# A transformer trunk on one core, split into two parts: all projections first, then attention and routing pair by pair in a new order

## The chip, the cores and the metric

The kernel runs on one core of a Trainium2 chip. The metric is the device time of one execution in microseconds (us), as the median of several runs. All times below are in us unless marked ns. TensorE multiplies matrices, VectorE and ScalarE work on elements, GpSimd here issues gathers of rows, and SyncE issues the other transfers, in the order of the program.

## The reference

One layer of a decoder is computed for a prompt of 1024 positions and for 8 sample rows of one position each, in float32. The model width is 1024.

```python
h = rmsnorm(x, norm_mix) * (1 + sc1) + sh1          # sc, sh, g: six rows of silu(c) @ w_ada + b_ada
qa, ka, va, ub, vb, xr, xg = split(h @ w_in)        # 1024 x 2560: q, k, v 512 each, the rest 256 each
ya = dilated attention of rmsnorm(q), rmsnorm(k), v # 8 heads x 64, three dilations, causal, relative bias
yb = spatial gating of ub by vb, chunks of 128
yc = gelu(xg) * linear recurrence of conv(xr)       # carries a state from one position to the next
x  = x + g1 * ([rms(ya) | rms(yb) | rms(yc)] @ w_out)
h2 = rmsnorm(x, norm_ffn) * (1 + sc2) + sh2
q2 = rmsnorm(h2 @ w_q)                              # 1024 x 2048: 8 heads, two halves of 128
for each head: the top 16 of 128 keys on each half, then the top 16 of their sums
               -> 128 experts e and gates w for every position
x  = x + g2 * sum_k w_k * gelu(h2 . u_tab[e_k]) * v_tab[e_k]   # tables of 16384 rows x 1024
```

## The kernel before, in words

**Tiles.** The prompt is cut into 8 tiles of 128 positions (0 to 7). The 8 sample rows are a ninth tile, `NT`. The trunk takes the tiles in the groups `(0, 1), (2, 3), (4, 5, NT), (6, 7)`. For each group `project(grp)` normalizes x, multiplies it with the five 512-column blocks of `w_in` (line 551, by `product`, lines 233 to 247), and makes queries, keys, values, the gating mixer and the recurrent mixer of it. It loads each block of `w_in` once for the group, so 4 x 20 loads of 512 KB. Keys and values go to tensors in device memory (`kT_d`, `vt_d`); queries and the mix stay on chip. Then `mix_and_route(grp, first)` runs attention for pairs of heads (`attention`, lines 591 to 625: logits at L606, weighted values at L623), the output projection with `w_out` (L695), the second norm, the router's product with `wq` (L728), the scores against the keys and the top 16 (`top16`). With the first group it also computes the remaining conditioning rows (`ada`, lines 185 to 213; the matmuls are L195 and L197), and with the third the sample rows' attention over their cache (`sample_attention`, lines 814 to 889).

**Experts.** Two ways lead through the experts. The tiles in `GATHER` fetch the rows of their 128 experts for each position: `peer_prompt` issues 128 fetches of 128 rows of `u_tab` and 128 of `v_tab`, each 512 KB, on GpSimd (L897); VectorE multiplies and adds them (L905, L914). The fetched rows take five buffers (`grow`). The tiles in `DENSE` go through all 16384 experts with matmuls in `dense()`, behind the trunk: 128 blocks of keys, each loading 512 KB of both tables, in 32 groups of four blocks (scores L1003, products L1019), with a table of gates that `gate_table` has built for each of these tiles (matmuls L805, ScalarE L804 and L807, VectorE L797) and stored to device memory.

**Order.** The code names neither semaphores nor times. A scheduler in front of the chip fixes one order of instructions for each engine, by the program's order as priority and by when operands are estimated to be ready. `pump` puts pieces of selection and gate tables of earlier dense tiles between the steps of attention and routing. The fetches of `peer_prompt` come last in the program and so fill what is free; a tile can be fetched once `select` has stored its experts. The next group's projection may run beside the routing of the group before. `Stream` objects hold the buffers: `Z` for projection, `R` for attention and routing together, each with two PSUM banks for products and some for the rest (`BANKS`), and both share seven buffers for weights (`WB`).

Of the kernel before, what the change touches and what calls it, by code (L numbers as in the profile page):

```python
# [23 lines left out]
GATHER = (0, 2, 6, 7)  # L24
DENSE = (1, 3, 4, 5)
GROUPS = ((0, 1), (2, 3), (4, 5, NT), (6, 7))
# [4 lines left out]
BANKS = dict(za=2, zs=1, ra=2, rs=2, g=1)  # L31
GST = 8
LK = 2
# [5 lines left out]
A4 = 3  # L39
WB = 7  # L40
# [20 lines left out]
def kernel(ctx: ExitStack, tc: tile.TileContext, I, O):  # L61
# [7 lines left out]
    mm = fctx.enter_context(tc.tile_pool(name="mm", bufs=1, space=PSUM))  # L69
    fc = fctx.enter_context(tc.tile_pool(name="fc", bufs=1))  # L70
    sm = fctx.enter_context(tc.tile_pool(name="sm", bufs=2))
    fr = fctx.enter_context(tc.tile_pool(name="fr", bufs=2))

    class Stream:


        def __init__(self, key, rows):
            self.key, self.rows = key, rows

        def ps(self, name="ps", kind="s"):  # L80
            return mm.tile([P, 512], F32, tag="p" + self.key + kind, name=name, bufs=BANKS[self.key + kind])

        def load_w(self, src):
            ws = []
            for j in range(4):
                w = fr.tile([P, 2, 512], F32, tag="w", name="w", bufs=WB)
                S.dma_start(w, src[j])
                ws.append(w)
            return lambda c: ws[c // 2][:, c % 2, :]

        def a2(self, name, dt=F32):
            return fr.tile([P, 512], dt, tag="a2" + self.key, name=name, bufs=self.rows)

        def junk(self):
            return fr.tile([P, D], BF, tag="a2" + self.key, name="junk", bufs=self.rows)

        def small(self, n, nm, bufs=2):
            return sm.tile([P, n], F32, tag=f"{nm}{n}{self.key}", name=nm, bufs=bufs)

    Z = Stream("z", 4)  # L100
    R = Stream("r", 4)

    def a4(name):
        return fr.tile([P, D], F32, tag="a4", name=name, bufs=A4)

    def c2(n, name):
        return fr.tile([P, 2, n], F32, tag="c2", name=name, bufs=2)

    def c1(n, name):
        return fr.tile([P, 2, n], F32, tag="c1", name=name, bufs=5)  # L110
# [5 lines left out]
    io_i = R.a2("io_i", I32)[:, :P]  # L116
    G.iota(io_i, pattern=[[1, P]], base=0, channel_multiplier=-1)
    V.tensor_scalar(ident, io_i, 0.0, None, op0=ALU.is_equal)
    tril = R.a2("tril")[:, :P]
# [10 lines left out]
    qgs = fc.tile([P, 1], F32, name="qgs")  # L130
    V.tensor_scalar(qgs, col("qg"), 0.125, None, op0=ALU.mult)
    bah = fc.tile([P, 4], F32, name="bah")
# [3 lines left out]
    xlast = fc.tile([P, 2, 3], F32, name="xlast")  # L136
    hlast = fc.tile([P, 2, 1], F32, name="hlast")
# [32 lines left out]
    cT = R.a2("cT")[:, :72].rearrange("p (c n) -> p c n", c=8)  # L170
    S.dma_start(cT, I["cT"])
    one32 = fc.tile([1, 32], F32, name="one32")
    V.memset(one32, 1.0)
    sc = fc.tile([P, 8, 32], F32, name="sc")
    sg_ = R.a2("se")[:, :72].rearrange("p (c n) -> p c n", c=8)
# [51 lines left out]
    def chunks(key, t):  # L227
        x = fr.tile([P, 8, wide(t)], F32, tag=f"hT{key}{wide(t)}", name="hT", bufs=2 if t < NT else 1)
# [21 lines left out]
    kgr = fc.tile([P, 64], F32, name="kgr")  # L250
    gnr = fc.tile([P, 256], F32, name="gnr")
    sp4 = fc.tile([P, 2], F32, name="sp4")
    nsp4 = fc.tile([P, 2], F32, name="nsp4")
    wsT = fc.tile([P, 4, P], F32, name="wsT")
    gw = fc.tile([P, 4, P], F32, name="gw")
    rb = fc.tile([33, 8, 8], F32, name="rb")
# [3 lines left out]
    def small_weights():  # L260
# [3 lines left out]
        nl, ab, u, z, z2, acc = (fc.tile([P, 2], F32, name=nm) for nm in ("nl", "ab", "lu", "lz", "lz2", "lacc"))  # L264
# [16 lines left out]
        wst = R.a2("wst").rearrange("p (g i) -> p g i", g=4)  # L281
# [8 lines left out]
    def bias_table():  # L290
        V.memset(rb, 1.0)
        rbs = fc.tile([32, 8], F32, name="rbs")
        S.dma_start(rbs, I["rel_bias"])
        V.tensor_copy(rb[:32], rbs[:, None, :].to_broadcast([32, 8, 8]))
        for q in range(3):
            ohq = R.a2("oh")[:33, :384]
            S.dma_start(ohq, I["oh"][:, q * 384:(q + 1) * 384])
            ps = R.ps("psr")
            T.matmul(ps[:8, :384], rb[:, 0, :], ohq, start=True, stop=True)
            rrow = R.a2("rrow")[:8, :384]  # L300
# [161 lines left out]
    def mixer_b(t, r, z, mix):  # L462
# [5 lines left out]
        if t == NT:  # L468
            S.dma_start(O["gv_s"], gv[:8])
            w0 = fr.tile([8, 8], F32, tag="w0", name="w0", bufs=1)  # L470
# [16 lines left out]
    def mixer_c(t, z, mix):  # L487
        if t == NT:
            S.dma_start(O["conv_s"][:, 2, :], z[:8, 0:256])
            S.dma_start(O["conv_s"][:, 0:2, :], I["state_conv"][:, 1:3, :])  # L490
            xps = fr.tile([P, 2, 4, 8], F32, tag="xps", name="xps", bufs=1)
            S.dma_start(xps[:, :, 0:3, :], I["state_convT"])
            xgs, h0 = (fr.tile([P, 2, 8], F32, tag=nm, name=nm, bufs=1) for nm in ("xgs", "h0"))
# [43 lines left out]
    qT, mix = {}, {}  # L537

    def project(grp):
        hT = {}  # L540
        for t in grp:
            r = rows_of[t]
            hT[t] = chunks("z", t)
            mix[t] = fr.tile([P, D], F32, tag="mix", name="mix", bufs=4)
            S.dma_start(mix[t][:r], x_src(t))
            normed_T(Z, t, r, mix[t], modT["sc1"], modT["sh1"], hT[t])
        for nb in (4, 0, 1, 3, 2):
            w = Z.load_w(I["w_in"][nb])
            for t in grp:
                r = rows_of[t]  # L550
                ps = product(Z, t, hT[t], w)
                z = Z.a2("z")
                A.copy(z[:r], ps[:r])
                if nb == 2:
                    if t == NT:
                        S.dma_start(O["v_s"], z[:8])
                        S.dma_start(v_d, z[:8])
                    else:
                        S.dma_start(O["v_p"][t * P:(t + 1) * P, :], z)
                        S.dma_start(vt_d[:, :, t, :].rearrange("h p e -> p h e"), z.rearrange("p (h e) -> p h e", h=4))  # L560
                elif nb == 0:
# [67 lines left out]
    def mix_and_route(grp, first):  # L629
        if first:  # L630
            ada(R, "g1")
# [550 lines left out]
```

## Time and profile before

| | us |
|---|---|
| median of three runs | 3331.42 |
| lowest, highest | 3325.81, 3339.45 |
| the profiled execution's own time | 3339.45 |
| its span, first to last instruction | 3337.4 |
| TensorE busy in the span | 2804.2 (84 %) |
| VectorE busy | 2542.5 (76 %) |
| GpSimd busy | 1405.2 (42 %) |
| ScalarE busy | 1197.8 (36 %) |
| moved by DMA | 952.57 MB, 285 GB/s on average |

In the rows below PE is TensorE's matmuls, PEld its weight loads, DVE VectorE, ACT ScalarE, POOL GpSimd and SPq SyncE's queue; `out<-in` are the program's names of tiles and tensors, and what stands behind a last arrow ended the idle time.

A busy share is an average over stages with different limits; matmuls are pipelined and their ends are modelled. The profile also gives the granted clock of TensorE as a share of its full speed (0.894 over the span).

### The profile page before, as it was taken

To read this page: it belongs to the slowest core of one execution; us is meant where nothing else is said; L and a number is where in the kernel's file an instruction comes from. 1 tells how busy PE (TensorE), PEld (TensorE's weight loads), DVE (VectorE), ACT (ScalarE), POOL (GpSimd) and SP (SyncE) were. 2 spreads that over 40 slices of the span, in tenths; PEclk is the share of its full clock that TensorE was granted. 3 is DMA by queue.
4 is the path that set the end of the run, shared out by engine and by line. 5 is a ranking of instruction groups with operands and counts; after the bars stand their busy time and mean duration, and the time that the engine had idled before them with its cause. 6 is when DMAs were issued, how large, how long until landed. Compare 5 with 4: busy or idle time off the path is not lost.

```text
span 3337.4 us, 36012 instructions
## 1 busy us (share of the span) xinstructions
PE 2804.2 (84%) x11152; PEld 1898.0 (57%) x11152; DVE 2542.5 (76%) x5342; ACT 1197.8 (36%) x2704; POOL 1405.2 (42%) x1046
## 2 busy tenths in 40 slices
PE   7989968856487788977768998989999989999989
PEld 3434445422145334555437876777777777777767
DVE  2216967897657788877798897888988888988974
ACT  4413566342137334575543221222222322222321
POOL 0000234414423543133423664666656466656540
PEclk9979988878577799898779999999999999999999
DMA  7665788938967888678886998999999899999983
GB/s 263 203 195 169 269 270 294 373 130 301 297 196 247 322 298 272 208 247 295 270 279 229 337 338 313 346 331 353 332 334 336 325 332 355 333 337 346 346 293 100
DMA packets 340670, 952.57 MB, mean 285 GB/s; under 512 B 35575, under 2 KB 118062, under 8 KB 338430
## 3 DMA queue, kind: packets, MB, share of 16 engines
q0 software_dynamic: 149760, 545.33, 46.3%
q1 hardware_dynamic: 190718, 404.95, 35.3%
q8 instruction: 88, 1.44, 0.2%
q14 instruction: 104, 0.85, 0.1%
HBM read 894.04 MB, written 60.85 MB: 286 GB/s over the span
## 4 chain that ended last, share of the span: by engine, by line
PE 27%; DMA 23%; issue 19%; DVE 14%; POOL 13%; ACT 4%; SPq 0%; POOLq 0%; DVEq 0%; ACTq 0%
POOL grow L897 13%; DMA grow<-in_peer_v,ge 9%; PE psz L238 7%; PE psG L805 4%; PE psO L1019 3%; PE psS L1003 3%; DMA grow<-in_peer_u,ge 3%; DVE acc L914 3%; DMA g_d<-st 3%; PE pso L623 2%; DVE grow L905 2%; PE pst L163 2%; PE lg L606 1%; DMA vt<-vt_d 1%; DMA vc<-in_cache_v 1%
## 5 line engine op out<-in xcount | busy, mean ns | idle before, releaser
L897 POOL DMA_INDIRECT grow<-in_peer_u,ge x520 | 697.3, 1341 | 1168.3 <-DVE grow L905 491.3
L897 POOL DMA_INDIRECT grow<-in_peer_v,ge x520 | 707.3, 1360 | 669.1 <-DVE acc L914 426.7
L914 DVE SCALAR_TENSOR_TENSOR acc<-grow,dot,acc 128x1024 f32<-128x1024 f32 x515 | 659.8, 1281 | 127.3 <-DMA grow<-in_peer_v,ge 120.9
L905 DVE SCALAR_TENSOR_TENSOR grow<-grow,gx 128x1024 f32<-128x1024 f32 x520 | 626.0, 1220 | 146.8 <-DMA grow<-in_peer_u,ge 116.2
L238 PE MATMUL psz<-w,hT 128*128 128x512 f32 x1408 | 673.5, 619 | 12.4 <-DVE hT L328 5.5
L238 PEld LDWEIGHTS psz<-w,hT 128*128 128x128 f32 x1408 | 261.8, 198 | 285.9 <-issue 261.9
L1019 PE MATMUL psO<-vh,ah 128*128 128x512 f32 x512 | 224.7, 439 | 125.4 <-DVE acc L1028 125.2
L972 ACT CAST vh<-v 128x1024 fp32r<-128x1024 f32 x128 | 125.3, 1049 | 504.7 <-PE psO L1019 502.6
L805 PE MATMUL psG<-o,oh 128*128 128x128 f32 x1024 | 204.7, 336 | 75.6 <-ACT st L807 66.0
L805 PEld LDWEIGHTS psG<-o,oh 128*128 128x128 f32 x1024 | 167.4, 229 | 148.5 <-ACT st L807 98.8
L797 DVE TENSOR_TENSOR oh<-iof,tr 128x1024 f32<-128x1024 f32 x128 | 156.4, 1224 | 98.6 <-PE psG L805 96.0
L972 ACT CAST ah<-a 128x512 fp32r<-128x512 f32 x128 | 79.7, 622 | 404.3 <-DVE a L1008 404.3
L972 ACT CAST uh<-u 128x1024 fp32r<-128x1024 f32 x128 | 135.0, 1055 | 232.5 <-PE psS L1003 229.8
L1019 PE MATMUL psO<-vl,ah 128*128 128x512 f32 x512 | 218.1, 426 | 0.0
L1019 PE MATMUL psO<-vh,al 128*128 128x512 f32 x512 | 216.1, 422 | 0.0
L1019 PE MATMUL psK<-vh,al 128*128 128x512 f32 x512 | 200.1, 391 | 9.8 <-DVE al L973 9.8
L804 ACT ACTIVATE o<-oh,tr 128x128 f32<-128x128 f32 x512 | 185.2, 400 | 45.7 <-PE psG L805 42.0
L1019 PEld LDWEIGHTS psO<-vh,ah 128*128 128x128 f32 x512 | 108.0, 211 | 164.6 <-DVE acc L1028 140.8
L1019 PE MATMUL psK<-vh,ah 128*128 128x512 f32 x512 | 199.8, 390 | 0.0
L1019 PE MATMUL psK<-vl,ah 128*128 128x512 f32 x512 | 199.7, 390 | 0.0
L973 DVE TENSOR_TENSOR ul<-u,uh 128x1024 fp32r<-128x1024 f32 x128 | 156.1, 1220 | 9.3 <-ACT uh L972 4.8
L973 DVE TENSOR_TENSOR vl<-v,vh 128x1024 fp32r<-128x1024 f32 x128 | 150.6, 1219 | 1.2 <-ACT vh L972 1.0
(369 smaller groups left out, 5024.2 us busy)
## 6 DMA issues: line engine op xcount, KB each, us to landing
u<-in_peer_uT SPq DMA_DIRECT2D x128, 512.0 KB
v<-in_peer_v SPq DMA_DIRECT2D x128, 512.0 KB
w<-in_w_in SPq DMA_DIRECT2D x80, 512.0 KB
w<-in_wq SPq DMA_DIRECT2D x64, 512.0 KB
g_d<-st SPq DMA_DIRECT2D x64, 512.0 KB
gc<-g_d SPq DMA_DIRECT2D x16, 2048.0 KB
w<-in_w_ada SPq DMA_DIRECT2D x48, 512.0 KB
w<-in_w_out SPq DMA_DIRECT2D x32, 512.0 KB
```

The costliest lines, as they stand in the source:

```text
L163: T.transpose(pv[:, c, :r], src[:, (c0 + c) * P:(c0 + c + 1) * P], ident[:r, :r])
L238: T.matmul(ps, xT[:, c, :], w(c), start=(c == 0), stop=(c == 7))
L797: V.tensor_tensor(oh, iof[:, None, None, :].to_broadcast([P, 2, OHB, P]), tt[:, 0:2, b * TB + n0:b * TB + n0 + OHB, None].to_broadcast([P, ...
L804: A.activation(o1, oh[:, 0, n0 % OHB + q, :], AF.Copy, scale=tt[:, 2, n:n + 1])
L805: T.matmul(ps[:, q * P:(q + 1) * P], oh[:, 1, n0 % OHB + q, :], o1, start=True, stop=True)
L897: G.indirect_dma_start(out=rt, out_offset=None, in_=tab, in_offset=bass.IndirectOffsetOnAxis(ap=idx, axis=0))
L905: V.scalar_tensor_tensor(rt, rt, 1.0, x, op0=ALU.mult, op1=ALU.mult, accum_out=w[:, k:k + 1])
L914: V.scalar_tensor_tensor(acc, rt, w[:, k:k + 1], acc, op0=ALU.mult, op1=ALU.add)
L972: A.copy(hi, x)
L973: eng.tensor_tensor(lo, x, hi, op=ALU.subtract)
L1003: T.matmul(ps[:, :n1 - n0], us_[x][:, j, :], xs_[j][y][:, n0:n1], start=(j == 0 and q == 0), stop=(j == 7 and q == 2))
L1019: T.matmul(ps, aa[x][:, t * P:(t + 1) * P], vv[y][:, hf * 512:(hf + 1) * 512], start=(k == 0 and (first or o not in keep)), stop=(k == 3 * ...
```

## The change

The trunk is split into two parts that have buffers and PSUM banks of their own.

The first part projects all nine tiles, one after the other, with the 20 pieces of `w_in` loaded once and kept in 20 buffers. All conditioning rows and the sample rows' attention are computed between the projections. Queries, and the half of the mix that the gating and recurrent mixers make, are now stored to device memory (`qT_d`, `mix_d`, `ya_d`) and loaded again by the second part.

The second part takes the groups in the order `(0, 1), (6, 7), (4, 5, NT), (2, 3)`. Attention has a stream of its own, `Y`. The banks are now two for logits and two for the rest of attention, one for routing products (two before), two for the rest of routing, one for gate tables. Keys, values and the router's keys have two buffers each (one before), the bias rows four (two before). The gathered tiles are 0 to 3 and the dense ones 4 to 7.

```diff
-GATHER = (0, 2, 6, 7)
-DENSE = (1, 3, 4, 5)
-GROUPS = ((0, 1), (2, 3), (4, 5, NT), (6, 7))
+GATHER = (0, 1, 2, 3)
+DENSE = (4, 5, 6, 7)
+GROUPS = ((0, 1), (6, 7), (4, 5, NT), (2, 3))
-BANKS = dict(za=2, zs=1, ra=2, rs=2, g=1)
+BANKS = dict(za=3, zs=3, xs=1, xv=1, aa=2, **{"as": 2}, ra=1, rs=2, g=1)
+TBB = 4
-A4 = 3
-WB = 7
+A4 = 4
+WZ = 6
+WB = 8
...
-    Z = Stream("z", 4)
-    R = Stream("r", 4)
+    first = Part("z")
+    Z = Stream(first, "z", 5)
+    X = Stream(first, "x", 4)
+    zp = first.fr
...
-    def project(grp):
+    def project(t):
...
         for nb in (4, 0, 1, 3, 2):
-            w = Z.load_w(I["w_in"][nb])
-            for t in grp:
+            if nb not in w_in:
+                w_in[nb] = Z.load_w(I["w_in"][nb], "wi", 20)
+            w = w_in[nb]
...
+                    qt = Z.a2("qT").rearrange("p (h n) -> p h n", h=4)
+                    transposes(Z, z, P, 4, lambda c0, pv: A.activation(qt, pv, AF.Copy, scale=qgs))
+                    S.dma_start(qT_d[t], qt)
...
+        S.dma_start(mix_d[t], mix[:r, 512:1024])
...
+    def mix_and_route(grp):
...
+        for t in grp:
+            mix[t] = fr.tile([P, D], F32, tag="mix", name="mix", bufs=4)
+            S.dma_start(mix[t][:rows_of[t], 512:1024], mix_d[t])
+            if t == NT:
+                S.dma_start(mix[t][:8, 0:512], ya_d)
+            else:
+                qT[t] = fr.tile([P, 4, P], F32, tag="qT", name="qT", bufs=2)
+                S.dma_start(qT[t], qT_d[t])
...
-            kT = fr.tile([P, D], F32, tag="kT", name="kT", bufs=1)
+            kT = fr.tile([P, D], F32, tag="kT", name="kT", bufs=2)
...
-            vt = fr.tile([P, NT, P], F32, tag="vt", name="vt", bufs=1)
+            vt = fr.tile([P, NT, P], F32, tag="vt", name="vt", bufs=2)
...
     ada(Z, "sc1")
     ada(Z, "sh1")
     small_weights()
+    project(0)
     bias_table()
+    project(1)
+    project(NT)
+    project(2)
+    sample_attention()
+    project(3)
+    ada(Z, "g1")
+    project(4)
+    ada(Z, "sc2")
+    project(5)
+    ada(Z, "sh2")
+    project(6)
+    project(7)
+    ada(Z, "g2")
+    first.close()
+    second = Part("r")
+    R = Stream(second, "r", 5)
+    Y = Stream(second, "a", 4)
...
     for i, grp in enumerate(GROUPS):
-        project(grp)
+        mix_and_route(grp)
+        pump(99)
         while late:
             now(select(late.pop()))
-        mix_and_route(grp, i == 0)
-        pump(99)
```

## Rows read from the trace of the kernel before

**Rows 1.** Stretches: busy us (count) of PE, PEld, DVE, ACT, POOL; clock, DMA, GB/s

```profile
core 0 of [0], span 3337.4 us
...
0.00:340.00 340.00, 298.73 (x997) 131.22 (x998) 115.51 (x601) 121.89 (x337) 0.63 (x6) 0.90 0.64 207
340.00:690.00 350.00, 283.56 (x1065) 160.49 (x1065) 283.35 (x855) 182.21 (x503) 143.29 (x117) 0.89 0.86 303
690.00:1040.00 350.00, 219.62 (x752) 104.92 (x751) 244.71 (x585) 123.08 (x314) 117.55 (x91) 0.72 0.70 227
1040.00:1355.00 315.00, 261.82 (x914) 130.19 (x912) 255.02 (x843) 136.42 (x394) 136.39 (x102) 0.88 0.84 290
1355.00:1716.00 361.00, 283.85 (x1287) 184.48 (x1286) 279.57 (x674) 213.25 (x619) 128.81 (x101) 0.85 0.77 254
1716.00:1771.00 55.00, 35.78 (x148) 29.02 (x149) 54.81 (x203) 30.52 (x38) 1.56 (x1) 0.79 0.78 260
1771.00:3188.00 1417.00, 1290.51 (x5437) 1051.64 (x5436) 1223.63 (x1485) 357.50 (x456) 853.69 (x612) 0.95 0.92 333
```

**Rows 2.** Fetches on GpSimd (L897): duration ns min/median/max, first and last start

```profile
L897 POOL DMA_INDIRECT grow<-in_peer_u,ge x520: 932/1299/4036, 358.7 to 3227.9; - x174
L897 POOL DMA_INDIRECT grow<-in_peer_v,ge x520: 932/1144/7060, 764.3 to 3242.3; - x174
```

**Rows 3.** SyncE's timeline, end of the span: start, duration, transfer

```profile
3204.97 0.34 SPq L923 DMA_DIRECT2D out_xp<-acc  x1
...
3296.68 0.34 SPq L954 DMA_DIRECT2D out_xs<-fin  x1
```

**Rows 4.** Waits from 340 to 1716: who for whom, us, times, longest

```profile
POOL grow L897 <- DMA ge<-e_d: 369.1, 2, 357.4
POOL grow L897 <- DVE grow L905: 320.5, 105, 32.0
```

**Rows 5.** DMA issues on the page: count, size

```profile
w<-in_w_in SPq DMA_DIRECT2D x80, 512.0 KB
```

**Rows 6.** TensorE's lines, 0 to 1716: count, busy us, mean ns, idle before

```profile
L238 PE MATMUL psz<-w,hT 128*128 128x512 f32 x1408 | 673.5, 619 | 12.4 <-DVE hT L328 5.5 <-DVE hss L337 3.3 <-DMA w<-in_w_in 2.4
...
L195 PE MATMUL psa<-w,sc 128*32 128x512 f32 x192 | 48.1, 755 | 14.7 <-DVE sc L180 10.9 <-DMA w<-in_w_ada 3.8
...
L163 PE MATMUL pst<-ident,mix 128*128 128x128 f32 (+1 forms) x144 | 31.0, 343 | 41.8 <-ACT hT L330 22.5 <-ACT mix L670 12.0 <-ACT mix L317 7.0
L872 PE MATMUL psv<-vc,pz 128*64 128x512 f32 (+1 forms) x32 | 30.0, 1070 | 32.2 <-DMA vc<-in_cache_v 31.9 <-ACT pz L865 0.3
L242 PE MATMUL psz<-w,hT 128*32 128x512 f32 x176 | 28.9, 642 | 3.1 <-DVE hss L337 3.1
...
L197 PE MATMUL psa<-brow,one 1*32 1x512 f32 x24 | 15.5, 732 | 0.0
...
L354 PE MATMUL psg<-xc,gw 128*128 128x128 f32 (+1 forms) x72 | 12.2, 315 | 10.5 <-DVE xc L350 10.5
```

**Rows 7.** The chain that ended last: start, duration, instructions

```profile
45.65 3.78 PE psz L238 x4
...
219.94 27.01 PE psz L238 x62
...
3248.79 21.76 PE psS L1003 x96
```

**Rows 8.** Logit matmuls (L606): duration ns, first and last start, shapes

```profile
L606 PE MATMUL lg<-kT,qT x192: 272/589/1219, 135.0 to 1465.2; 64*128 64x512 f32 x96, 64*128 64x128 f32 x32, 64*128 64x256 f32 x32, 64*128 64x384 f32 x32
```

**Rows 9.** Lines of all engines, 340 to 1716, columns as before

```profile
L905 DVE SCALAR_TENSOR_TENSOR grow<-grow,gx 128x1024 f32<-128x1024 f32 x256 | 309.9, 1218 | 51.1 <-DMA grow<-in_peer_u,ge 49.5 <-DMA gx<-h_d 0.8
...
L914 DVE SCALAR_TENSOR_TENSOR acc<-grow,dot,acc 128x1024 f32<-128x1024 f32 x148 | 188.8, 1276 | 30.7 <-DMA grow<-in_peer_v,ge 29.6
...
L730 ACT COPY q<-psz 128x512 f32<-128x512 f32 (+1 forms) x28 | 16.3, 582 | 50.4 <-PE psz L238 38.9 <-PE psz L246 6.5 <-DVE tkw L379 3.7
...
L697 DVE TENSOR_TENSOR tmp<-psz,g1r 128x512 f32<-128x512 f32 (+1 forms) x14 | 9.6, 685 | 9.3 <-PE psz L238 8.5 <-DMA g1r<-mods_g 0.5 <-PE psz L246 0.4
```

More of the change, by code (lines that the diff above doesn't have):

```diff
@@ L227, in chunks @@
     def chunks(key, t):
-        x = fr.tile([P, 8, wide(t)], F32, tag=f"hT{key}{wide(t)}", name="hT", bufs=2 if t < NT else 1)
+        x = (zp if key == "z" else R.fr).tile([P, 8, wide(t)], F32, tag=f"hT{wide(t)}", name="hT", bufs=2 if t < NT else 1)
         if t == NT:
@@ L247, in product @@
         return ps
[L250 to L256, printed above, removed]
+    kgr = zp.tile([P, 64], F32, name="kgr")
+    gnr = zp.tile([P, 256], F32, name="gnr")
+    sp4 = zp.tile([P, 2], F32, name="sp4")
+    nsp4 = zp.tile([P, 2], F32, name="nsp4")
+    wsT = zp.tile([P, 4, P], F32, name="wsT")
+    gw = zp.tile([P, 4, P], F32, name="gw")
+    rb = zp.tile([33, 8, 8], F32, name="rb")
     rb_d = dpool.tile([8, 1152], F32, name="rb_d")
@@ L616, in attention @@
             h_ = 2 * hp + hh
-            nmx = sm.tile([P, 1], F32, tag="nmx", name="nmx", bufs=4)
+            nmx = R.fr.tile([P, 1], F32, tag="nmx", name="nmx", bufs=4)
             A.activation(nmx, mx[hh], AF.Copy, scale=-1.0)
             A.activation(p_[hh][:, :nk], p_[hh][:, :nk], AF.Exp, bias=nmx, accum_out=sums[:, h_:h_ + 1])
-            pT = [R.a2("pT").rearrange("p (c q) -> p c q", c=4) for _ in range(0, t + 1, 4)]
-            transposes(R, p_[hh][:, :nk], P, t + 1, lambda c0, pv: A.copy(pT[c0 // 4][:, :pv.shape[1], :], pv))
+            pT = [Y.a2("pT").rearrange("p (c q) -> p c q", c=4) for _ in range(0, t + 1, 4)]
+            transposes(Y, p_[hh][:, :nk], P, t + 1, lambda c0, pv: A.copy(pT[c0 // 4][:, :pv.shape[1], :], pv))
             for c in range(t + 1):
@@ L627 @@
     tv = {}
-    def mix_and_route(grp, first):
-        if first:
-            ada(R, "g1")
+    def mix_and_route(grp):
+        fr = R.fr
         pt = [t for t in grp if t < NT]
-        if NT in grp:
-            sample_attention(mix[NT])
-        sums = {t: sm.tile([P, 8], F32, tag="sums", name="sums", bufs=4) for t in pt}
+        mix = {}
+        for t in grp:
+            mix[t] = fr.tile([P, D], F32, tag="mix", name="mix", bufs=4)
+            S.dma_start(mix[t][:rows_of[t], 512:1024], mix_d[t])
+            if t == NT:
+                S.dma_start(mix[t][:8, 0:512], ya_d)
+            else:
+                qT[t] = fr.tile([P, 4, P], F32, tag="qT", name="qT", bufs=2)
+                S.dma_start(qT[t], qT_d[t])
+        sums = {t: fr.tile([P, 8], F32, tag="sums", name="sums", bufs=4) for t in pt}
         u0 = 896 - P * pt[-1]
         for hp in range(4):
-            tb = [fr.tile([P, D], F32, tag="tb", name="tb") for _ in range(2)]
+            tb = [fr.tile([P, D], F32, tag="tb", name="tb", bufs=TBB) for _ in range(2)]
             for hh in range(2):
@@ L812, in gate_table, with sample_attention @@
             yield
-    def sample_attention(mix):
+    def sample_attention():
         n_d = dpool.tile([8, 8], F32, name="n_d")
@@ L1086 @@
             now(gate_table(t))
+    second.close()
     fctx.close()
```

219 lines of the change are left out of this document (108 added, 111 removed).

## The prediction

> **What bounds the kernel now.** I read the stretches first, cut where the program changes its work, because the kernel has two halves that are limited differently. The reader should see three things in [rows 1]. From 0 to 340 TensorE is busy for 298.7 us while GpSimd, which fetches expert rows, does nothing. From 340 to 1716 (the rest of the trunk) nothing is saturated: TensorE is at 81, 63, 83 and 79 % in the four stretches, VectorE at 81, 70, 81 and 77 %, the DMA at 0.70 to 0.86. From 1771 to 3188 (the dense experts) TensorE is at 91 %, VectorE at 86 % and the DMA at 0.92 with 333 GB/s.
>
> The count in brackets behind POOL is that of row fetches. There are 1040 [rows 2]: 1024 for the four gathered tiles and 16 for the sample rows. Until 1716 411 of them are done (117 + 91 + 102 + 101), so 613 tile fetches are left to the dense half. They start at 358.7 [rows 2], when the first pair is routed. In the dense half 612 of them take from 1771 to 3188, 2.32 us each; the sample's output goes out at 3296.7 [rows 3], and the span ends at 3337.4. So the fetches end only just before the dense products, and a kernel that moves fetches from the trunk into the dense half soon ends with the fetches.
>
> Then the waits: GpSimd waits 369.1 us for expert indices, most of it for the first, and 320.5 us for VectorE to free a row buffer [rows 4]. The fetches are paced by VectorE's order, not by their own engine. The last views were the loads, the chain that ended last, and TensorE's lines.
>
> **The change, part by part.** All sums are in us of the profiled execution, whose span stands 6 above the median of the three runs (its own time 8 above).
>
> *Weights kept on chip.* Of 80 loads of 512 KB [rows 5], 60 go. What the matmuls of these lines waited for them is 2.4 in all [rows 6], so no more is won directly. Their 31.5 MB would be worth 94 at the 333 GB/s of the dense half, if the DMA bounded the trunk; at a share of 0.70 to 0.86 it doesn't. The queries and half of the mix of every tile are now stored and read again, 8.4 MB or 25 at that rate: hidden under the same free share, 25 if that cover were gone. I take 0 for both together, with ends of -96 and +25.
>
> *First part.* Now all nine projections, the twelve halves of the conditioning and the sample attention run before any routing. TensorE's work after the first product at 45.65 [rows 7]: 640 of the 1408 records of projections and routing, at 27.01/62 = 0.436 each [rows 7], 279; eight halves of conditioning that are not yet done, (48.1 + 15.5) x 8/12 = 42; the sample's products, 5/11 of 28.9, 13; 20 transposes a tile and 12 for the sample, 172 x 31.0/144 = 37; the gates of the recurrent mixer 12; the sample attention's products 30 [rows 6]. That is 413. If TensorE never waits the part ends at 459; at the 88 % of the first 340 us, at 515. I take 92 %: 45.65 + 449 = 495. ScalarE and VectorE fit beneath it (121.9 and 115.5 in the first 340). The moved loads (32 of conditioning weights, 40 of the key and value cache and of the query rows) lie in the same SyncE queue as the projections' stores, where the DMA share was 0.64.
>
> *The seam.* The second part's buffers lie where the first part's were. The kernel before has one such place, the 55 us between trunk and dense half, with TensorE busy for 35.8 of them [rows 1]: 19 lost. I take 19, with ends of 0 and 55. What waits there first are the loads of keys, values, bias rows and mix; behind them in SyncE's queue stand the output weights, and TensorE waits for all of it.
>
> *First fetch.* Before, it went out 224 after the first logits at 135.0 [rows 2, 8]. In that time lay the 42 of conditioning, which move away: 182 remain. So the first fetch comes at 495 + 19 + 182 = 696, which is 337 later than before. Nothing covers that: no other tile is routed earlier.
>
> *Rest of the trunk.* TensorE was busy for 283.6 + 219.6 + 261.8 + 283.9 = 1049 from 340 to 1716 [rows 1]. What moves ahead of it: products of six tiles, 480 x 0.436 = 209; their and the sample's transposes, 132 x 0.215 = 28; the sample's products 13, gates 9, sample attention 30. 760 remain. Some 25 of it (the next pair's first logits) fits into the waits of the first pair. In the three stretches without the sample attention TensorE was busy for 829 of 1026, 81 %. The second part has separate banks and buffers for attention and two buffers for keys and values, so that the next pair's attention can fill waits of routing; but the projections that filled such waits before are gone. I take 86 %: 735/0.86 = 855, and the trunk ends at 1551 instead of 1716, 165 earlier. At 81 % it is 1603, at 95 % 1470.
>
> *One bank for routing products, two before.* Copying a query product takes 582 ns and scaling an output product 685 ns [rows 9]; if each of the 54 stood in TensorE's way it would be 36 x 0.58 + 18 x 0.69 = 33. Transposes and key products of the block before stand ready to fill it, so I take 0 beyond the 86 %. The Trainium skill, Perfetto Trace Analysis, section Matmuls, says that independent groups should rotate through different banks, so that the copy of one overlaps the matmuls of the next. By it the trunk would end up to 33 later; no row here shows one bank.
>
> *Fetches in the trunk.* The last pair's stretch, with two gate tables, gave one fetch in 361/101 = 3.57 us; the three stretches without the sample attention gave 3.15 on average, (331 + 315 + 361)/320 [rows 1, 2]. The last two pairs now have two tables each, so I take 3.55: 855/3.55 = 241 fetches instead of 411. VectorE could hardly do more. It was busy for 1063 from 340 to 1716, of which fetches took 411 x 1.3 = 534 [rows 1, 9]. Of the other 529 I estimate that 100 moves ahead (the first 340 us, with two tiles projected and routed, show 115.5). 430 + 241 x 1.3 = 743 in 855 is 87 %, more than any stretch of the trunk shows.
>
> *Dense half and end.* The dense half was 3337.4 - 1716 = 1622. Where fetches had ended, 96 score products took 21.76 [rows 7], so a group of 192 takes 43.5, while 1622/32 = 50.7 is the average; two groups ran so, and with fetches to the end the half is 14 longer, 1636. It takes 1 fetch in its first 55 and (1636 - 55)/2.32 = 683 in the rest. Needed are 1024 - 241 = 783. The 99 left over come alone: GpSimd's and VectorE's 1.3 a fetch bound one below [rows 2, 9], the 2.32 above; I take 1.5, together 149. Behind them come the sample rows, which before lay beneath the dense half: 92 from the store of the last gathered tile to that of the sample, under full traffic [rows 3]. I take 50, with ends of 30 and 92.
>
> **Sum.** 1551 + 1636 + 149 + 50 = 3386, 49 above the span. Against the median of 3331 that is 3380. What the trunk saves (165) is less than what the fetches ask for at the end (149 + 50 + 14).
>
> **The rivals.** With T for the end of the trunk and n for the fetches done by then, the end is T + 1636 + 1.5 (340 - n) + 50.
>
> *Faster: the next pair's attention fills the waits of routing.* With TensorE at 95 % the trunk ends at 1470. If the fetches keep the spacing of 340 to 690, (690 - 359)/117 = 2.83, n is 774/2.83 = 273 and the end 3257, against the median 3251. For it: separate banks and buffers, no sample attention in between (the stretch at 63 %). Against it: VectorE would need (430 + 355)/774, over 100 %; with VectorE at 95 % n is 235 and the end 3314, against the median 3308. It decides at a spacing of 3.55 if the trunk ends before 1468, at 2.83 if before 1643. Chance 0.33.
>
> *No difference: the fetches catch up.* At the average spacing of 3.15 and T = 1551, n is 271 and the end 3341, 4 above the span. It needs 91 % of VectorE. Chance 0.16. That the loads saved bring nothing because they were hidden is part of the forecast already.
>
> *Clearly slower: VectorE stays at the 81 % of the better stretches.* n = (0.81 x 855 - 430)/1.3 = 202, the end 3444, against the median 3438. It counts to the forecast's side, together 0.51.
>
> **How the numbers follow.** The likeliest case is the forecast, 3380; its own range is 3348 to 3438, from spacings of 3.25 to 4.2. The whole range goes from 3260 (the faster rival nearly in full) to 3460 (a trunk of 1603 besides). Half a per cent of 3331 is 17, about what three runs can tell from no change: faster by more than that 0.33, within it 0.16, slower 0.51.
>
> **What would show it.** In the trace after: no fetch before about 690 (if before 620, the first part was shorter); the dense half's first load at about 1550; 240 fetches before it; fetches still going when TensorE has stopped, with the sample rows last. If the fetches end before the dense products, my spacing was wrong, and so is the prediction. If the dense half is longer than 1650 or shorter than 1600, something in it changes that I have missed. If TensorE is over 92 % busy in the second part, the faster rival has it.

## The result, and the profile after

The changed kernel takes 3484.41 us (median of four runs, 3483.18 to 3501.12) against 3331.2 of the kernel before (four runs): a ratio of 1.0469, 95% interval 1.0431 to 1.0508. It is slower, as forecast, but by 153 and not by 49; 3484 lies 24 above the top of the range. The profiled execution has a span of 3482.6, and the sum that was made against the span gave 3386.

The stretches after, cut at the first logits (526), the first fetch (735), the dense half's first load (1632) and the end of TensorE's work; they answer to [rows 1], with the columns as there; of the dense half the table shows 1657 to 3238.

```profile
core 0 of [0], span 3482.6 us
core 0: us, PE busy (x) PEld busy (x) DVE busy (x) ACT busy (x) POOL busy (x), PEclk, DMA share, GB/s
0.00:526.00 526.00, 443.57 (x1392) 188.72 (x1392) 157.82 (x551) 189.63 (x413) 0.63 (x6) 0.93 0.39 133
526.00:735.00 209.00, 176.51 (x666) 94.61 (x666) 100.72 (x546) 92.06 (x264) 0.57 (x1) 0.84 0.50 163
735.00:1632.00 897.00, 694.00 (x2950) 426.28 (x2950) 736.00 (x2111) 507.80 (x1493) 318.08 (x250) 0.83 0.73 250
1657.00:3238.00 1581.00, 1435.67 (x6058) 1168.97 (x6058) 1371.76 (x1902) 415.94 (x530) 938.27 (x665) 0.95 0.91 331
...
3258.00:3482.00 224.00, 0.08 (x1) 0.00 (x0) 153.33 (x132) 0.21 (x1) 142.08 (x110) 0.51 0.81 281
```

The last line is the result in one row: for 224 us TensorE does nothing, and GpSimd still issues 110 fetches. TensorE itself stops at 3258, 73 earlier than before. In the rest of the trunk (735 to 1632) TensorE is busy for 694 of 897, 77 %, and VectorE for 736, 82 %.

The fetches on GpSimd after, with the columns of [rows 2]:

```profile
L917 POOL DMA_INDIRECT grow<-in_peer_u,ge x520: 932/1436/15509, 734.4 to 3448.2; - x174
L917 POOL DMA_INDIRECT grow<-in_peer_v,ge x520: 932/1265/2629, 1173.0 to 3460.6; - x174
```

The end of SyncE's timeline after, answering to [rows 3]:

```profile
3429.01 0.34 SPq L943 DMA_DIRECT2D out_xp<-acc  x1
...
3479.93 0.34 SPq L974 DMA_DIRECT2D out_xs<-fin  x1
```

GpSimd's waits after, from 735 to 1632, answering to [rows 4]:

```profile
POOL grow L917 <- DMA ge<-e_d: 733.2, 1, 733.2
POOL grow L917 <- DVE grow L925: 198.1, 41, 68.2
POOL grow L917 <- DVE acc L934: 107.5, 33, 11.6
```

And on the page after, the loads that stand in [rows 5]:

```profile
w<-in_w_in SPq DMA_DIRECT2D x20, 512.0 KB
```

The first fetch waits for the first indices until 733, where it was 357; from then on it waits for VectorE, as before. The sample's output goes out at 3480, behind everything.

### The profile page after: what moved, and what is told of

Its sections match the earlier page's. It is cut to its first block, busy times and chain, and to the rows that moved or that the text cites. A ratio compares the mean times of both kernels' runs of the same rounds, so it can differ in the third digit from the quotient of the medians.

```text
span 3482.6 us, 36002 instructions
## 1 busy us (share of the span) xinstructions
PE 2769.6 (80%) x11152; PEld 1894.6 (54%) x11152; DVE 2559.5 (73%) x5342; ACT 1213.8 (35%) x2713; POOL 1421.1 (41%) x1046
## 4 chain that ended last, share of the span: by engine, by line
PE 24%; issue 24%; DMA 17%; POOL 17%; DVE 12%; ACT 5%; SPq 0%; POOLq 0%; DVEq 0%; ACTq 0%
POOL grow L917 17%; PE psz L250 10%; DMA grow<-in_peer_v,ge 8%; PE psG L824 4%; DMA g_d<-st 2%; PE pst L175 2%; DMA grow<-in_peer_u,ge 2%; PE lg L622 2%; DVE acc L934 1%; PE pso L639 1%; DVE grow L925 1%; ACT st L826 1%; PE psO L1039 1%; DVE tkw L391 1%; DMA w<-in_w_ada 1%
## 5 line engine op out<-in xcount | busy, mean ns | idle before, releaser
L917 POOL DMA_INDIRECT grow<-in_peer_u,ge x520 | 716.7, 1378 | 1440.0 <-DMA ge<-e_d 733.2
L250 PE MATMUL psz<-w,hT 128*128 128x512 f32 x1408 | 663.4, 610 | 8.3 <-DVE tmp L716 6.5
L824 PEld LDWEIGHTS psG<-o,oh 128*128 128x128 f32 x1024 | 175.9, 239 | 165.5 <-ACT st L826 106.1
```

What stands on the lines that cost most here:

```text
L250: T.matmul(ps, xT[:, c, :], w(c), start=(c == 0), stop=(c == 7))
L824: T.matmul(ps[:, q * P:(q + 1) * P], oh[:, 1, n0 % OHB + q, :], o1, start=True, stop=True)
L917: G.indirect_dma_start(out=rt, out_offset=None, in_=tab, in_offset=bass.IndirectOffsetOnAxis(ap=idx, axis=0))
```

## The experiments

The theory with which I began (A): the fetches now end last, they start 376 us later, and what the split saves on TensorE can't show. The rivals: the split doesn't shorten the trunk at all (B), or the order of pairs, the single routing bank or the start alone is the loss. Seventeen kernels were run, each beside the kernel before on the same chip; the ratios are against that one. Its median there was 3322 to 3331, so a difference between two changed kernels that were run at different times can be off by some 9 us. The table gives medians and, read from each trace, the first fetch, the end of the trunk T (the dense half's first load), the fetches issued until T, the end of TensorE's work and the last fetch. Before and after are in it for comparison.

| kernel | us | ratio, 95% | first fetch | T | fetches to T | TensorE ends | last fetch |
|---|---|---|---|---|---|---|---|
| before | 3331 | | 359 | 1716 | 411 | 3331 | 3242 |
| after | 3484 | 1.043 to 1.051 | 734 | 1632 | 250 | 3258 | 3461 |
| e1 before, no fetch | 2873 | 0.862 to 0.867 | | 1443 | | 2860 | |
| e2 after, no fetch | 2930 | 0.879 to 0.884 | | 1503 | | 2924 | |
| e3 before, late start | 3364 | 1.009 to 1.015 | 688 | 1646 | 317 | 3253 | 3338 |
| e4 early route | 3411 | 1.025 to 1.029 | 404 | 1810 | 482 | 3399 | 3171 |
| e5 e2, old order | 2915 | 0.871 to 0.880 | | 1483 | | 2905 | |
| e6 e2, shared banks | 2989 | 0.893 to 0.902 | | 1560 | | 2982 | |
| e7 after, old order | 3472 | 1.038 to 1.047 | 729 | 1626 | 253 | 3252 | 3454 |
| e8 before, sample later | 3369 | 1.006 to 1.018 | 358 | 1760 | 446 | 3363 | 3210 |
| e9 before, thin VectorE | 3349 | 1.005 to 1.010 | 355 | 1757 | 512 | 3333 | 2827 |
| e10 after, thin VectorE | 3313 | 0.993 to 0.999 | 735 | 1673 | 330 | 3308 | 3127 |
| e11 before, select later | 3360 | 1.006 to 1.013 | 362 | 1746 | 418 | 3351 | 3245 |
| e12 e2, norm ahead | 2876 | 0.861 to 0.868 | | 1451 | | 2873 | |
| e13 after, norm ahead | 3438 | 1.030 to 1.039 | 687 | 1586 | 250 | 3215 | 3416 |
| e14 e4, norm ahead | 3444 | 1.031 to 1.040 | 409 | 1830 | 472 | 3436 | 3219 |
| e15 e10, norm ahead | 3270 | 0.981 to 0.990 | 685 | 1624 | 330 | 3254 | 3074 |
| e16 before, four stores | 3323 | 0.995 to 1.000 | 365 | 1716 | 425 | 3309 | 3186 |
| e17 e13, four stores | 3423 | 1.025 to 1.032 | 687 | 1574 | 254 | 3207 | 3395 |

### Without the fetches: e1, e2, e5, e6, e12

In these five no expert row is fetched; the gathered tiles and the sample rows store x1 alone. The edit, in both kernels:

```diff
-        e, w, x = routed(t, [P, P], lambda d: d)
-        S.dma_start(x, h2_d[t])
-        acc = experts(x, e, w, P)
-        finish(t, acc, grow)
+        x = grow("x1o")
+        S.dma_start(x, x1_d[t])
+        S.dma_start(O["xp"][t * P:(t + 1) * P, :], x)
```

> The kernel before without any fetch of expert rows: the four gathered tiles and the sample rows leave out their experts and only store x after the first residual. Both theories: the dense half takes 32 x 43.5 = 1392 and some 50 to start, the trunk 1500 to 1650 without 411 fetches on VectorE, so 2950 to 3100 in all. It is the partner of the next run.

> The changed kernel without any fetch, with the same left out as in the run before. Theory A (the fetches start late and end last; the split itself shortens the trunk): faster than its partner by 60 to 150, as the trunk of the changed kernel was 84 shorter with fetches. Theory B (the split trunk is itself no better: one bank for routing products, the new order, less to interleave): within 20 of its partner, or slower.

e1 is faster than its forecast, in the trunk and in all. Without fetches the split kernel is 57 slower, and its trunk ends at 1503 against 1443. So the part of A falls by which the split saves time in the trunk. What shortens it in the pair before and after (1716 to 1632) is that fewer fetches lie in it. The fetches cost the trunk 273 for 411 before, and 129 for 250 after: 0.66 and 0.52 each. In e3, further down, which is the kernel before with a later start, it is (1646 - 1443)/317 = 0.64, if e1's trunk is taken for it too.

Stretches of e2, cut as those of after:

```profile
core 0 of [0], span 2930.5 us
...
0.00:526.00 526.00, 447.43 (x1392) 189.51 (x1392) 157.94 (x551) 189.45 (x413) 0.64 (x6) 0.93 0.39 132
526.00:734.00 208.00, 176.91 (x666) 94.98 (x666) 97.22 (x516) 91.98 (x264) 0.00 (x0) 0.84 0.53 175
734.00:1503.00 769.00, 669.05 (x2950) 409.52 (x2950) 462.41 (x1766) 499.72 (x1490) 0.00 (x0) 0.88 0.41 125
```

From 734 on, the same 2950 matmuls take 769 where they took 897 with fetches, and TensorE is at 87 %. Of the 128, 25 are TensorE's own work (694 against 669 us, at a mean granted clock of 0.83 against 0.88), the other 103 are waiting. e5 is e2 with the tiles in the groups of before.

```diff
-GATHER = (0, 1, 2, 3)
-DENSE = (4, 5, 6, 7)
-GROUPS = ((0, 1), (6, 7), (4, 5, NT), (2, 3))
+GATHER = (0, 2, 6, 7)
+DENSE = (1, 3, 4, 5)
+GROUPS = ((0, 1), (2, 3), (4, 5, NT), (6, 7))
```

> The changed kernel without fetches (as in the run of that kind before), with pairs and tiles as in the kernel before: (0,1), (2,3), (4,5), (6,7), of each of the first two pairs one tile dense. It keeps the two parts. Theory C (the second part waits at the seams between pairs, because nothing is left to fill the selection of two dense tiles at once; the new order makes it worse): trunk 20 to 50 shorter than 1503, in all 2880 to 2910. Theory D (order is of no account; the split or the one bank costs the 60): 2920 to 2940.

The new order costs 20 of the trunk and 15 of the time: a part, not the 57, and between the two forecasts. In e6 the routing products no longer have a bank of their own; they rotate through three banks with the rest of routing.

```diff
-BANKS = dict(..., ra=1, rs=2, g=1)
+BANKS = dict(..., rs=3, g=1)
-        ps = st.ps("psz", "a")
+        ps = st.ps("psz", "s" if st.key == "r" else "a")
```

> The changed kernel without fetches, where routing products take turns in three banks with the other routing results, instead of one bank of their own and two for the rest. If the one bank costs: 20 to 40 less than 2930. If the copy is covered, as I predicted: within 10 of 2930.

That is 59 slower, nearly all of it behind 735 (825 there instead of 769), and neither forecast had it. So sharing three banks is no cure; what a second bank for the products alone would bring was not run. The Trainium skill says that independent groups of matmuls should rotate through different banks (Perfetto Trace Analysis, section Matmuls). The rotation of e6, over banks that the products share with smaller results, lost 59, so it tests that sentence only in this form.

What then are the 57? TensorE's waits in e2 up to 526, just ahead of its first logits at 528 (who for whom, us, times, longest):

```profile
PE pst L175 <- ACT mix L329: 32.8, 9, 4.2
PE psa L207 <- DVE sc L192: 11.8, 1, 11.8
```

In e12 each tile is normalized before the projection of the tile ahead of it. Its edit, and TensorE's waits up to its first logits at 477:

```profile
PE psa L207 <- DVE sc L192: 11.7, 1, 11.7
...
PE pst L175 <- ACT mix L329: 4.1, 2, 3.9
```
```diff
-    def project(t):
...
+    def prepare(t):
         r = rows_of[t]
         hT = chunks("z", t)
...
         normed_T(Z, t, r, mix, modT["sc1"], modT["sh1"], hT)
+        ready[t] = hT, mix
+
+    def project(t):
...
+        n = TURN.index(t) + 1
+        if n < len(TURN):
+            prepare(TURN[n])
+        hT, mix = ready.pop(t)
```

> The changed kernel without fetches, where each tile of the first part is normalized ahead of the projection of the tile before it. TensorE waits nine times at the start of a tile in the first part, 32.8 in all, for ScalarE's normalized rows. If this is part of what the split costs: the trunk 25 to 35 shorter, 2895 to 2910. If these waits are covered elsewhere: 2920 to 2935.

Nine times, once a tile, TensorE had waited for ScalarE to write a normalized tile. With that gone the first logits come at 477 instead of 528, and the time falls by 53, to that of e1; the forecast had 20 to 35. The waits give 29 of it (32.8 to 4.1). Another 17 are TensorE's own work in the part (447 to 430 us busy), at a mean granted clock of 0.96 instead of 0.93. Nearly all of the split's own price was in the first part: projecting one tile after the other leaves no other work under the norm of the next. In e1 TensorE waits 3 us in all for these rows. The new order (15) and the norms (53) were not taken out together; if they add up, they are more than the 57, and something else in the split gains a little.

### The start of the fetches: e3, e7, e4, e8, e11

e3 is the kernel before with only the gathered and dense tiles exchanged, so that the first gathered tile is routed with the second group:

```diff
-GATHER = (0, 2, 6, 7)
-DENSE = (1, 3, 4, 5)
+GATHER = (2, 3, 6, 7)
+DENSE = (0, 1, 4, 5)
```

> The kernel before with one thing changed: tiles 2, 3, 6, 7 are fetched and 0, 1, 4, 5 are dense, so that the first tile to fetch is routed at about 700 instead of 359. The work is the same. Theory A: 100 fetches fewer at the end of the trunk (about 310), a dense half that ends near 3350 and fetches that end behind it, 3400 to 3480. Theory B: the start of the fetches doesn't matter, 3310 to 3365.

```profile
core 0 of [0], span 3359.0 us
...
688.00:1646.00 958.00, 689.77 (x2640) 369.84 (x2640) 736.19 (x1965) 402.73 (x1124) 403.21 (x317) 0.81 0.82 276
...
3253.00:3359.00 106.00, 0.00 (x0) 0.00 (x0) 63.95 (x63) 0.21 (x1) 51.25 (x40) 0.52 0.71 246
```

A start at 688, 46 before that of after, costs 40 in the time against the kernel before beside it (3324), and not 153. That is in B's range, at its upper end, though the fetches now end behind TensorE, as A had it. Trunk and dense half end nearly as in after (1646 and 3253), but 317 fetches are done by then, one in 3.02 us against 3.59, and 40 are left behind TensorE instead of 110. The difference, 70 fetches, took 118 us (224 less 106). So a late start alone is the smaller part of the 153. The larger one, as the rows read, is that the split trunk, once the fetches have begun, has less room for them on VectorE. With 1.25 of VectorE's time for each fetch [rows 9], its other work is 424 of the 897 in after (736 - 250 x 1.25), and 340 of the 958 in e3. The sum is the same in both: VectorE is busy for 258 up to the first fetch in after and for 342 in e3, so 682 with what follows. While no fetch runs e3 does 84 more of that work than after, in 46 us less. No run moves this work alone; e9 and e10, further down, bear it out.

e7 is the changed kernel, with fetches, in the order of before (diff as in e5).

> The changed kernel with fetches, with pairs and tiles as in the kernel before (fetched 0, 2, 6, 7). The first fetch stays at about 734. Theory C: the trunk ends 20 to 50 earlier than 1632, but fetches still end last: 3440 to 3475. Theory D: 3475 to 3500.

13 faster, 8 if each is set against the kernel before beside it, and the trunk ends 6 earlier where theory C had 20 to 50: the order is a small term here, if it is one. e4 routes the first pair before the other tiles are projected, so the fetches start early again; six tiles are then projected with kept weights, then routed in pairs.

```diff
-    project(0)
-    bias_table()
-    project(1)
-    ...
+    project(0, 1)
+    bias_table()
+    ada(Z, "g1")
+    ...
+    after_group(0, GROUPS[0])     # attention and routing of the first pair
+    project(NT)
+    project(2)
+    ...
```

> The changed kernel with the first pair projected, attended and routed first, as in the kernel before; then the projections of the other tiles with the input weights kept on chip, then the other three pairs as in the changed kernel. 20 loads of input weights more than in the changed kernel. Theory A: the first fetch at 350 to 400, fetches run under the projections, about 400 of them by the end of the trunk at 1600 to 1680, and the dense products end last: 3230 to 3320, faster than both. Theory B: 3430 to 3520, like the changed kernel.

That is 74 faster than after and between the two forecasts: A had 3320 at most. The fetches end at 3171, and TensorE is the bound again, at 3399; its trunk has grown to 1810 with 482 fetches in it. So an early start takes the fetches off the end, and they are paid for in the trunk. The Trainium skill says that stretches with different busiest engines can gain when they are interleaved (Perfetto Trace Analysis, section Optimization Strategy). e4 against after agrees with it, by 74; e4 against before shows that it isn't a matter of the fetches' start alone.

e8 and e11 asked of the kernel before whether less crowding in its trunk pays. e8 puts the sample attention behind the attention of its group; e11 moves the first selection into the queue of pieces that fill waits.

```diff
-        if NT in grp:
-            sample_attention(mix[NT])
         ...
+        if NT in grp:
+            sample_attention(mix[NT])
```
```diff
+            elif i == 0:
+                pending.append(select(t))
```

> The kernel before with one step moved: the sample rows' attention is issued behind the attention of tiles 4 and 5 instead of ahead of it. In the kernel before TensorE is 63 % busy in the stretch from 690 to 1040 that holds it. If that step is what stands in the way there: the trunk 20 to 60 shorter, 3280 to 3325. If the stretch waits for something else: 3315 to 3345.

> The kernel before with the selection of tile 0 put among the pieces that run between the attention steps of the next pair, so that the first fetch goes out at about 435 instead of 359. If both ends only need balancing (before: products end 34 behind the sample's output; with the start at 688 the fetches end about 100 behind the products): 3300 to 3320, faster than before by 0.3 to 0.9 %. If a later start only loses: 3335 to 3350.

Both are slower, by 1.2 and 1.0 %, more than either forecast of theirs had. In e11 the first fetch still went out at 362, so it doesn't test a later start; why it is slower stays open.

### Who paces the fetches: e9, e10

In both, VectorE's two operations on a fetched row work on 8 of its 1024 columns, so the other 1016 columns are left out of the experts' products; every row is still fetched.

```diff
-V.scalar_tensor_tensor(rt, rt, 1.0, x, ..., accum_out=w[:, k:k + 1])
+V.scalar_tensor_tensor(rt[:, 0:8], rt[:, 0:8], 1.0, x[:, 0:8], ..., accum_out=w[:, k:k + 1])
-V.scalar_tensor_tensor(acc, rt, w[:, k:k + 1], acc, ...)
+V.scalar_tensor_tensor(acc[:, 0:8], rt[:, 0:8], w[:, k:k + 1], acc[:, 0:8], ...)
```

> The kernel before with all 1040 fetches, but VectorE multiplies and adds 8 of the 1024 columns of each fetched row (so the experts' sums are left out). If a fetch costs the trunk by its VectorE time: the trunk ends near 1443, its length without fetches, dense groups take near 43.5, about 2870 to 2960 in all. If it costs by its transfers: the trunk stays above 1600 and the dense groups near 50, 3150 or more.

> The same with the changed kernel. VectorE time: trunk near 1503, 2930 to 3020 in all, slower than its partner by 40 to 70, as without any fetch. Transfers: 3200 or more, with fetches behind the dense products.

Stretches of e9 in the dense half, cut where its fetches end:

```profile
...
1771.00:2827.00 1056.00, 932.13 (x3919) 751.16 (x3920) 476.86 (x1349) 273.79 (x349) 539.04 (x527) 0.95 0.97 372
2827.00:3333.00 506.00, 505.95 (x2227) 418.25 (x2225) 206.87 (x246) 139.01 (x179) 1.06 (x2) 1.00 0.36 120
```

The same of e10:

```profile
...
1700.00:3127.00 1427.00, 1275.54 (x5369) 1030.60 (x5370) 645.72 (x1780) 369.55 (x472) 712.41 (x702) 0.96 0.97 369
3127.00:3308.00 181.00, 177.87 (x777) 146.06 (x775) 77.90 (x97) 45.28 (x58) 0.94 (x1) 0.99 0.35 115
```

The kernel before doesn't gain, its median is 23 higher: its fetches end 415 earlier, but 512 of them now lie in the trunk, which ends 41 later, and TensorE ends at 3333 as before. Its fetch stream was not its bound. The changed kernel gains 172 and is then faster than e9: its fetches end at 3127, and TensorE, at 3308, is the bound. So the time of after is set by the fetch stream as VectorE lets it go, 2.62 us a fetch from 734 to 3461; with thin work, 2.30. That the fetches would still end behind the dense products, as e10's forecast by transfers had it, is not so. In the trunk alone, from the first fetch to T, the spacing falls from 3.30 to 2.74 in the kernel before and from 3.59 to 2.84 in the changed one: most of the changed kernel's lag goes with VectorE's work on the rows, which fits the reading of e3. The price of a fetch in the trunk is not VectorE's time, though: (1757 - 1443)/512 is 0.61 in e9, against 0.66, and (1673 - 1503)/330 is 0.52 in e10, as in after.

### With the norms ahead, and fetches: e13, e14, e15

e13 is after with the edit of e12, e14 the kernel e4 with it, e15 the kernel e10 with it (and its thin VectorE work, as there).

> The changed kernel with its fetches, each tile normalized before the projection of the tile ahead of it. Without fetches this edit moved the end of the trunk from 1503 to 1451 and the time by 53. Theory A (the fetches end last, and their stream only starts earlier): the first fetch moves from 734 to about 685, the trunk ends near 1585 with the same 250 fetches before it, TensorE ends near 3210, and the time falls by about 49 to some 3435, still slower than before by 3 %. Theory B (the waits of the first part were the loss): the time falls by much more than 50, towards 3340. Theory C (the fetch stream, once it sets the end, is paced by the dense half and by VectorE as a whole, so an earlier start is given back): under 20 us.

> The three-part kernel (pair (0,1) projected and routed first, then the projections of the others with kept weights, then the other pairs), with each of the later projections normalized ahead. In the three-part kernel TensorE set the end (3399 of 3405), and its middle part projects 6 of the 8 tiles. Theory A (TensorE's waits in the middle part show in the end, fetches or none): 6/8 of the 52 us, some 35 to 40, so 3370 to 3376, still 1 % slower than before. Theory B (the fetches beside the middle part hold it, whatever the order of its norms): within 10 us of 3411.

> The changed kernel with VectorE's two operations on a fetched row cut to 8 of the 1024 columns (so its output of the experts isn't the reference's) and each tile normalized ahead. The cut alone gave 3313, with TensorE last at 3308 and the last fetch at 3127. Theory A (TensorE sets the end there, so its waits in the first part show in full): about 50 less, 3262, 2 % faster than before. Theory B (the transfers pace the end): 10 less at most.

e13 comes out as A had it: everything from the first fetch on moves by 43 to 47, the same 250 fetches lie before T, and the time falls by 46. In e15 TensorE sets the end, its end moves by 54, and the time falls by 43 to 1.5 % below the kernel before. e14 misses both forecasts: 33 slower than e4, with T some 20 and TensorE's end 37 later. In its middle part other waits stand where those for the norms were (for ScalarE's copies of products, 31 us from 400 to 1200). That work which is put ahead delays what was there, where fetches share VectorE with the projections, would explain it; no run tests that.

### The price of a fetch in the trunk: e16, e17

Of TensorE's waits that of the gate tables' products for ScalarE's copies grows most with fetches: 34 in e2, 66 in after, 125 in e10, from 735 to the end of the trunk. The copies wait for the stores of 512 KB that empty their buffers (3, 35 and 100). e16 is the kernel before with four such buffers for three, e17 is e13 with four; each gives up one weight buffer.

```diff
-            sts = [... name="st", bufs=3) for _ in range(2)]
+            sts = [... name="st", bufs=4) for _ in range(2)]
```

> The kernel before with four store buffers for the gate tables where it has three, paid for with one weight buffer of seven. In the kernel before the copies into these buffers waited 41 us in the trunk for the stores of 512 KB to DRAM (no wait of that kind over 4 us without fetches), and the table's matmuls waited 66 us for the copies. Theory A (the transfers of the fetches hold the trunk through these stores): the trunk ends 25 to 40 us earlier, some ten fetches fewer before it, and since TensorE ends last here the time falls to 3290 to 3310, 1 % faster. Theory B (the transfers hold something else instead as soon as this wait is gone: the same bytes must move): within 10 us of the kernel before.

> The changed kernel, normalized ahead, with four store buffers of the gate tables for three, paid for with one weight buffer of eight. With three it took 3438. The copies waited 35 us for the stores in the changed kernel. As the fetches end last, TensorE's gain doesn't show by itself. Theory A (a shorter trunk has fewer fetches before it, and those cost 2.4 us each in the dense half or 2 after it): the trunk ends about 25 earlier with 7 to 10 fetches fewer, so the time falls by 0 to 15. Theory B (the store buffers also free VectorE and GpSimd, which wait behind them): 25 or more, to 3410.

The wait in the kernel before, from 340 to 1716, and TensorE's first waits of e16, from 340 to 1704:

```profile
PE psG L805 <- ACT st L807: 66.0, 52, 6.2
...
PE psv L872 <- DMA vc<-in_cache_v: 34.2, 11, 13.9
PE pst L163 <- ACT x L317: 27.6, 5, 15.3
PE psG L805 <- ACT st L807: 26.6, 42, 0.8
PE pst L163 <- ACT hT L330: 25.4, 4, 11.8
```

The wait fell from 66 to 27, and the trunk still ends at 1716, now with 425 fetches: 0.64 each, as before. Other waits took its place, as B had it. The median is 5 lower, within 0.5 %. e17 ends the trunk 12 earlier and is 15 faster than e13; the wait there fell from 67 to 42. The 15 is A's upper end (21 if each is set against the kernel before beside it), but not by A's way: the trunk was to end 25 earlier with 7 to 10 fetches fewer, and it has 254 for 250.

But for e15 and those without fetches, which leave work out, no version beat the kernel before by more than half a per cent.

## Why the prediction was wrong, step by step

**What held.** The direction, and the mechanism: the fetches end last, behind TensorE, with the sample rows at the very end. These sizes held too, the measured ones in brackets: a fetch spacing of 3.55 in the rest of the trunk (897/250 = 3.59), 241 fetches (250), a dense half of 1636 (1632 to 3258 is 1626), 115 fetches left with the sample's 16 (110), 20 loads of the input weights. e6 doesn't contradict that the single bank costs nothing, but it tests no second one for the products alone.

**What failed.** The 97 between 3386 and 3482.6 go over four terms: +38 before the first fetch, +43 in the rest of the trunk, -10 in the dense half, +26 behind it.

*Rest of the trunk, "I take 86 %: 735/0.86 = 855".* This is the step that failed. TensorE's work was 694, 41 less than my 735, but its share was 77 %: 897. The 86 % is what the split trunk reaches without fetches (87 % in e2). I had seen 81 % in stretches with fetches in them, put it down to dependencies, and let the separate banks and the second buffers for keys and values raise it. But without fetches the kernel before is at 88 % there as well (968 us busy in 1103, e1), so dependencies were not what held it at 81 %. What holds the share down is the fetches, half a microsecond each, 129 for 250. So the 165 that I had the trunk save were not there to save: it ends 84 earlier with its fewer fetches, and 60 later than before when both have none. My lower bound, 81 % or 1603, was still too high.

*First fetch, "182 remain".* The conditioning that moves away was priced at 42 of the 224 between first logits and first fetch. Only 16 went (526 to 734 is 208). The stretch before, and the same stretch after:

```profile
135.00:359.00 224.00, 201.59 (x677) 91.53 (x676) 94.43 (x512) 85.45 (x258) 0.30 (x1) 0.87 0.56 179
L195 PE MATMUL psa<-w,sc 128*32 128x512 f32 x107 | 27.1, 751 | 2.6 <-DMA w<-in_w_ada 2.6
L623 PE MATMUL pso<-pT,vt 128*64 128x128 f32 x48 | 11.5, 362 | 5.1 <-DMA vt<-vt_d 2.9 <-ACT pT L621 2.1
L606 PE MATMUL lg<-kT,qT 64*128 64x128 f32 (+1 forms) x32 | 8.9, 450 | 1.3 <-DVE mx L611 1.3
```
```profile
526.00:734.00 208.00, 176.51 (x666) 94.61 (x666) 99.72 (x538) 92.06 (x264) 0.00 (x0) 0.84 0.50 164
L639 PE MATMUL pso<-pT,vt 128*64 128x128 f32 x168 | 30.7, 324 | 4.1 <-ACT pT L637 4.1
L622 PE MATMUL lg<-kT,qT 64*128 64x512 f32 (+3 forms) x70 | 27.7, 609 | 13.2 <-DMA kT<-kT_d 9.4 <-DVE mx L627 3.8
```

The conditioning did go (27 in L195, 46 with its smaller matmuls), and with it 24 of projections of the next pair. In their place came attention of the next pair, some 49 with its transposes: 168 products with values where there were 48, and 70 logits where there were 32. I had let 25 of that run there, in waits. TensorE's work fell by 25, its idle time rose from 22 to 31. So the room was taken by other work; how much of that work stands in the way of the first fetch, no run shows. In e7, where the next pair has shorter rows of keys, the stretch is 200 (529 to 729).

*First part and seam, 495 + 19.* The first logits came at 526, 12 later; of the 38 before the first fetch 12 lie here and 26 in the step above. That is small, but e12 and e13 show what lay in it: nine waits for the norm, which I had spread into "92 %". Without them, and at the higher granted clock that goes with it (0.95 to 0.96 for 0.93), the logits come 48 earlier.

*Fetches behind the dense half, 149 + 50.* They took 224. 110 fetches from 3258 to 3461 are 1.85 each, where I took 1.5.

**The rivals.** The faster one wanted TensorE at 95 %; even without fetches it is at 87 %. "Clearly slower" was right about its condition, VectorE at 82 % where it said 81 %, but in a stretch 42 longer, so 250 fetches fit where it had 202. "No difference" wanted a spacing of 3.15, and it was 3.59. Put into the prediction's formula, the measured T and count give 1632 + 1636 + 1.5 x 90 + 50 = 3453: the rest is the slower fetches at the end (39), less the 10 of the dense half.

**What stays open.** What a fetch takes from TensorE in the trunk. It isn't VectorE's time on the row (e9, e10), and not the table stores alone (e16). Part of it is TensorE's own work at a lower granted clock: 25 of the 128 between e2 and after, and 78 of the 273 between e1 and the kernel before (1270 and 1348 us busy up to T, at 0.92 and 0.85). The rest is waiting. That the 512 KB of each fetch delay many small transfers and stores a little would fit, with DMA at 0.73 in this stretch against 0.41 in e2; no run took the bytes away and left the fetches.

## What to carry to other kernels

When a stream that runs in the background ends close to the main work, write down its first and last time and its spacing in every stage: a change that delays its start has to win back the delay in that stream, and not on the busiest engine. Take an engine's share in a stage with the background stream off as well as on before you forecast that more buffers will raise it; the loss may be the stream. And before you count work that moves out of a stage as time won there, see which work stands ready to take its place, and which waits open where it goes.

## What I had not expected

Taking nearly all of VectorE's work on fetched rows away made the kernel before no faster, but slower by 0.75 % (e9, 1.0050 to 1.0100). The fetches then crowd into the trunk, 512 instead of 411, where each costs 0.6 us, and leave the dense half without any for its last 506 us. In that stretch TensorE ran at a granted clock of 1.00, the upper of its two levels (2.4 GHz), and was busy all the time. In the traces the two sides cancel: the trunk ends 41 later, and what follows takes 39 less (1576 for 1615). The 23 between the medians are not in them, as the trace of the kernel before is of its slowest run.
